# Eight scaled copies of h queued behind the last square of h, at the seam into layer 1's feed-forward

## The chip, the cores and the metric

The kernel runs on one core of a Trainium2 chip. The metric is device time in microseconds, the median of several executions; one further execution was recorded by the hardware profiler and is the source of all times inside the kernel. The engines are named as in the profile: PE (TensorE's matmuls) and PEld (its weight loads), DVE (VectorE), ACT (ScalarE), POOL (GpSimd), SP (SyncE, which issues most DMAs).

## The reference

Two layers over x of 512 rows by 1024 channels. Layer 0 is a convolution module and a feed-forward, layer 1 a windowed attention and a feed-forward; each is added to the running sum h, and a norm ends it. What matters here is the feed-forward of layer 1, with D = 1024 and a hidden width of 2816:

```python
def rmsnorm(x, g):
    xf = x.astype(jnp.float32)
    xf = xf * lax.rsqrt(jnp.mean(xf * xf, axis=-1, keepdims=True) + EPS)
    return (xf * g.astype(jnp.float32)).astype(x.dtype)

def swiglu_ffn(x, w_up, w_down):
    gate, up = jnp.split(x @ w_up, 2, axis=-1)
    return (jax.nn.silu(gate) * up) @ w_down
...
            h = h + attn @ w_o[j]
        h = h + swiglu_ffn(rmsnorm(h, norm_ffn[l]), ffn_w_up[l], ffn_w_down[l])
    return rmsnorm(h, norm_final)
```

## The kernel before

Activations lie transposed: h is eight tiles, h0 to h7, of 128 channels by 512 rows. A product in float32 precision is made of three fast ones (mm3): weights and activations are both split into a rounded high part and a low remainder, and high x high (L356), the weight's high x the activation's low (L357) and the weight's low x the activation's high (L358) are added up in a PSUM bank.

Weights come in chunks of 512 KB in the order of a fixed plan. SP loads a chunk into a raw tile (four of them), ACT casts it to its high part (L273, out whi), DVE subtracts to get the low part (L276, out wlo). A chunk is split up to three uses ahead, into four pairs of tiles, so a cast can wait for PE to be done with an older chunk. Meanwhile sums of weight blocks are made by accumulating DMAs that GpSimd issues (L268).

The norm's factor is applied late: x is h times the norm's gain, and the factor of each row multiplies the result. So the seam from attention to the feed-forward goes like this. The output projection leaves its result in banks and DVE adds it to h (L1410), tile after tile. For each finished tile `Rows.on_h` makes x and adds to the sum of squares: ACT writes the high part of x (L510), DVE the remainder (L511), ACT the square of h (L463), DVE adds it to the squares so far (L467). `Rms.step1` then has PE sum the squares over channels (L477), DVE scale the sum (L479), GpSimd raise it to the power -1/2 (L481) and DVE lay it on a diagonal (L484); `spread` has PE broadcast it (L503).

In layer 1 six of eleven pairs of up-projection tiles are made with seven block products in place of eight. Pair 0 is not: `plain_pair` runs it in four chunks of 24 products, each over half of x's eight tiles. Beside it, `Rows.sums` prepares what the later pairs read: ACT writes eight unrounded scaled copies of h into two tiles f (L726), four to each, and GpSimd makes from them T1 = B11 - B12 (from the first four), T3 = B22 - B12, T2 and T4 (L732). ACT and DVE split each into high and low parts (L518 or L515, and L519 or L516), and the block products read those parts under the name rows.

The order of instructions on each engine is not that of the program text: a planner lays it out when the kernel is built, by a simulated timeline, and each engine then runs its queue strictly in that order. `tc.issue_after(ins)` binds whatever the block under it puts on the engine of `ins` to come after `ins` in that order; it adds no wait on the chip.

The two lines of the seam in which the change lies are `nc.scalar.square(sq, t)` in `Rms.add` and `nc.scalar.mul(f[i // 4][:, i % 4, :], h[i], col(self.gain, i))` in `Rows.sums`.

Of the kernel before, what the change touches and what calls it, by code (L numbers as in the profile page):

```python
# [199 lines left out]
def hybrid_trunk(ctx: ExitStack, tc: tile.TileContext, xT, W, prm_in, wdw_in, sinks, relb, onehot, fin, lead, out):  # L200
    nc = tc.nc
# [10 lines left out]
    def uid(s):  # L212
        ctr[0] += 1
        return f"{s}{ctr[0]}"
# [4 lines left out]
    def quad(dt=F32R):  # L219
        return quads.tile([P, 4, 512], dt, tag="quad", name=uid("quad"))  # L220

    def temp():
        return tmp.tile([P, 512], F32, tag="tmp", name=uid("tmp"))
# [171 lines left out]
    h = [hT[:, i, :] for i in range(KT)]  # L395
# [53 lines left out]
    def col(name, i):  # L449
        c = PARAM_COLS[name] + i  # L450
        return prm[:, c:c + 1]


    class Rms:
# [5 lines left out]

        def add(self, t):
            sq = temp()[:, 0:self.w]
            nc.scalar.square(sq, t)  # L463
            if self.acc is None:
                self.acc = sq
            else:
                self.eng.tensor_add(sq, self.acc, sq)  # L467
                self.acc = sq
# [44 lines left out]
    def split(dst, src, negative=False):  # L513
        if negative:
            nc.scalar.mul(dst[0], src, -1.0)  # L515
            nc.vector.scalar_tensor_tensor(dst[1], src, -1.0, f32(dst[0]), op0=ALU.mult, op1=ALU.subtract)  # L516
            return
        nc.scalar.copy(dst[0], src)  # L518
        nc.vector.tensor_sub(dst[1], src, f32(dst[0]))  # L519
# [190 lines left out]
    class Rows:  # L710
# [12 lines left out]
        def sums(self):  # L723
            f = [quad(F32) for _ in range(2)]
            for i in range(KT):
                nc.scalar.mul(f[i // 4][:, i % 4, :], h[i], col(self.gain, i))  # L726
            b11, b12, b21, b22 = (x[:, :, s] for x in f for s in HALF)
            t1 = self.pool.tile([P, 1024], F32, tag="sum", name=uid("t1"), bufs=1).rearrange("p (k s) -> p k s", k=4)

            for name, t, f, a, b in (("T1", t1, nc.gpsimd.tensor_sub, b11, b12), ("T3", b12, nc.gpsimd.tensor_sub, b22, b12),  # L730
                                     ("T2", b11, nc.gpsimd.tensor_add, b12, b11), ("T4", b21, nc.gpsimd.tensor_sub, b11, b21)):
                f(t, a, b)  # L732
                yield
                both = quads.tile([P, 2, 4, 256], F32R, tag="quad", name=uid("rows"))
                self.block[name] = [both[:, a] for a in range(2)]
                split(self.block[name], t, name == "T2")
# [483 lines left out]
    if True:  # L1220
# [162 lines left out]
        for part in range(2):  # L1383
            for g in range(2):
# [23 lines left out]
                for m in range(4):  # L1408
                    i = g * 4 + m
# [98 lines left out]
```

## Time and profile before

| | us |
|---|---|
| median of 3 executions | 1071.57 |
| lowest and highest | 1064.79, 1073.39 |
| the profiled execution | 1072.48 |
| its span | 1070.1 |
| PE, busy | 1054.9 |
| DVE, busy | 748.5 |
| ACT, busy | 554.1 |
| POOL, busy | 432.8 |

The span runs from the first to the last instruction of the profile; the rest of the execution's time lies around it. Times in rows count from the span's start. A row of the timeline gives start, duration, engine, source line, operation, what is written and read with shapes, a count, and in brackets the engine's idle time before it with what ended it. A row of the waits gives who waited for whom, total time, number of waits, longest one. A row of a line's own view gives a count, shortest, median and longest duration in ns, and the first and last start.

### The profile page before, as it was taken

How to read it: one execution, taken by the hardware profiler on the slowest of the kernel's cores; microseconds unless marked ns; L12 is line 12 of the kernel's file. 1: busy time of each engine (PE TensorE's matmuls, PEld its weight loads, DVE VectorE, ACT ScalarE, POOL GpSimd, SP SyncE). 2: the span in 40 equal slices, each digit the busy share in tenths (PEclk: the TensorE clock that was granted, in tenths of full speed). 3: DMA queues.
4: the chain of work that ended last, by engine and by line, in shares of the span. 5: the costliest groups of instructions: out<-in, count | busy, mean ns of one | idle time of the engine just before them, and what ended most of it. 6: DMA issues, size and time to landing. Idle time of an engine off the chain costs nothing.

```text
span 1070.1 us, 16002 instructions
## 1 busy us (share of the span) xinstructions
PE 1054.9 (99%) x5878; PEld 917.0 (86%) x5878; DVE 748.5 (70%) x1159; ACT 554.1 (52%) x968; POOL 432.8 (40%) x523
## 2 busy tenths in 40 slices
PE   9999999999999999999999999998999999999996
PEld 7888889999988888888888877777989899898985
DVE  3999988977777644444436466487767778768867
ACT  3887888755565333222343565474544355444543
POOL 3999998710321312211212344123532415315401
PEclk9999999999999999999999999998999999999998
DMA  9238046565556777676766444455989655545532
GB/s 356 86 98 98 3 141 214 178 230 184 177 183 191 236 203 211 169 211 190 189 188 188 138 109 137 118 158 158 277 229 332 213 188 179 157 156 177 180 118 79
DMA packets 52059, 187.92 MB, mean 176 GB/s; under 512 B 6188, under 2 KB 12493, under 8 KB 51277
## 3 DMA queue, kind: packets, MB, share of 16 engines
q1 hardware_dynamic: 44924, 162.74, 46.4%
q0 software_dynamic: 6336, 23.07, 12.6%
q8 instruction: 46, 0.75, 0.3%
q10 hardware_dynamic: 720, 1.10, 0.3%
q14 instruction: 33, 0.26, 0.1%
HBM read 181.64 MB, written 51.38 MB: 218 GB/s over the span
## 4 chain that ended last, share of the span: by engine, by line
PE 96%; DVE 2%; ACT 1%; issue 1%; DMA 1%; POOL 0%; SPq 0%
PE bank L356 19%; PE bank L357 19%; PE bank L358 19%; PE bank L906 10%; PE bank L848 9%; PE bank L388 5%; PE bank L354 4%; PE bank L389 3%; PE bank L1304 1%; PE bank L1346 1%; PE bank L1333 1%; PE bank L1004 1%; DMA both<-in_lead_dram 1%; PE bank L894 1%; PE bank L1461 0%
## 5 line engine op out<-in xcount | busy, mean ns | idle before, releaser
L276 DVE TENSOR_TENSOR wlo<-raw,whi 128x1024 fp32r<-128x1024 f32 x219 | 299.7, 1371 | 175.2 <-ACT whi L273 174.1
L273 ACT CAST whi<-raw 128x1024 fp32r<-128x1024 f32 x219 | 229.6, 1049 | 311.7 <-PE bank L357 199.7
L357 PE MATMUL bank<-quad,whi 128*128 128x512 f32 (+1 forms) x1008 | 349.8, 347 | 3.9 <-DVE quad L511 3.9
L356 PE MATMUL bank<-quad,whi 128*128 128x512 f32 (+1 forms) x1008 | 350.1, 348 | 0.0
L358 PE MATMUL bank<-quad,wlo 128*128 128x512 f32 (+1 forms) x1008 | 349.4, 347 | 0.0
L357 PEld LDWEIGHTS bank<-quad,whi 128*128 128x128 f32 x1008 | 191.5, 190 | 27.5 <-DVE quad L511 4.3
L356 PEld LDWEIGHTS bank<-quad,whi 128*128 128x128 f32 x1008 | 191.6, 190 | 24.8 <-issue 1.6
L358 PEld LDWEIGHTS bank<-quad,wlo 128*128 128x128 f32 x1008 | 191.5, 190 | 23.9 <-issue 0.6
L948 POOL TENSOR_TENSOR pr<-pr,pr 128x256 f32<-128x256 f32 x208 | 156.9, 812 | 6.6 <-ACT pr L947 6.6
L955 DVE SCALAR_TENSOR_TENSOR bank<-apad,wdw,bank 128x256 f32<-128x256 f32 x248 | 112.4, 484 | 3.4
L947 ACT ACTIVATE pr<-apad,wdw 128x256 f32<-128x256 f32 x208 | 98.2, 501 | 14.8 <-POOL pr L948 13.0
L906 PE MATMUL bank<-quad,w 128*128 128x256 f32 x448 | 98.7, 380 | 0.0
L906 PEld LDWEIGHTS bank<-quad,w 128*128 128x128 f32 x448 | 84.9, 190 | 11.8 <-DVE bank L955 0.2
L388 PE MATMUL bank<-quad,whi 128*128 128x512 f32 x212 | 75.9, 398 | 0.0
L268 POOL DMA_DIRECT2D sum<-in_W_dram x22 | 18.3, 833 | 123.0 <-DMA sum<-in_W_dram 122.8
L822 POOL TENSOR_TENSOR up<-up 128x256 f32<-128x256 f32 x40 | 44.2, 1114 | 43.0 <-DVE up L768 41.4
L268 POOL DMA_DIRECT2D sum<-sum x22 | 18.0, 818 | 105.8 <-DMA sum<-in_W_dram 104.3
L389 PE MATMUL bank<-quad,wlo 128*128 128x256 f32 x212 | 59.3, 280 | 0.0
L467 POOL TENSOR_TENSOR tmp<-tmp,tmp 128x256 f32<-128x256 f32 (+1 forms) x28 | 27.0, 963 | 79.1 <-ACT tmp L463 62.8
L848 PE MATMUL bank<-wlo,fhi 128*128 128x512 f32 x140 | 55.1, 393 | 0.0
L356 PE MATMUL bank<-rows,whi 128*128 128x256 f32 x192 | 54.6, 285 | 0.0
L358 PE MATMUL bank<-rows,wlo 128*128 128x256 f32 x192 | 54.3, 283 | 0.0
(220 smaller groups left out, 1603.3 us busy)
## 6 DMA issues: line engine op xcount, KB each, us to landing
raw<-in_W_dram SPq DMA_DIRECT2D x187, 512.0 KB, 3.8
sum<-in_W_dram SPq DMA_DIRECT2D x44, 512.0 KB, 5.4
raw<-sum SPq DMA_DIRECT2D x44, 512.0 KB, 3.9
sum<-in_W_dram POOLq DMA_DIRECT2D x22, 512.0 KB, 6.6
sum<-sum POOLq DMA_DIRECT2D x22, 512.0 KB, 6.4
w<-in_W_dram SPq DMA_DIRECT2D x14, 512.0 KB, 9.0
fd<-fs SPq DMA_DIRECT2D x1, 3072.0 KB, 34.1
h<-in_xT_dram SPq DMA_DIRECT2D x8, 256.0 KB, 8.4
```

The lines of the kernel that those rows point to most:

```text
L273: on_act = nc.scalar.copy(hi, src).ins
L276: latest[:] = [on_act, lo_engine[0].tensor_sub(lo, src, f32(hi)).ins]
L356: nc.tensor.matmul(out, w[0], x[0], start=start, stop=False)
L357: nc.tensor.matmul(out, w[0], x[1], start=False, stop=False)
L358: nc.tensor.matmul(out, w[1], x[0], start=False, stop=stop)
L388: nc.tensor.matmul(first[2], first[0], first[1], start=start, stop=False)
L389: nc.tensor.matmul(second[2], second[0], second[1], start=False, stop=stop)
L848: nc.tensor.matmul(out, x, w[:, ws], start=first and e == 0 and i == 0, stop=e == 1 and i == 2, skip_group_check=True)
L906: mm = nc.tensor.matmul(self.pb[:, w * W2:(w + 1) * W2], w1_of(ct, w, k), x[k] if x else xg[k][:, tok], start=k == 0, stop=k == KT - 1)
L947: on_act = nc.scalar.mul(pr, a[:, j:j + W2], tap(j))
L948: on_pool = nc.gpsimd.tensor_add(pr, acc, pr)
L955: on_dve = nc.vector.scalar_tensor_tensor(yt if i == nd - 1 else c, src, tap(i), c if i else self.shift, op0=ALU.mult, op1=ALU.add)
```

## The change

`Rms.add` keeps the square that it has just issued, so that after all eight tiles `squared` is the square of h7. `Rows.sums` issues its eight copies with that square as their predecessor on ACT. The operations and their operands are the same.

```diff
         def add(self, t):
             sq = temp()[:, 0:self.w]
-            nc.scalar.square(sq, t)
+            self.squared = nc.scalar.square(sq, t).ins
...
         def sums(self):
             f = [quad(F32) for _ in range(2)]
             for i in range(KT):
-                nc.scalar.mul(f[i // 4][:, i % 4, :], h[i], col(self.gain, i))
+                with tc.issue_after(self.rms.squared):
+                    nc.scalar.mul(f[i // 4][:, i % 4, :], h[i], col(self.gain, i))
```

## The prediction

> **What bounds the kernel now.** I read the page first, then the list of waits, the windows around the one long wait, and then the timelines of the engines there. From the page, the span and instructions, TensorE's share, and the chain that ended last:
>
> ```profile
> span 1070.1 us, 16002 instructions
> PE 1054.9 (99%) x5878; PEld 917.0 (86%) x5878; DVE 748.5 (70%) x1159; ACT 554.1 (52%) x968; POOL 432.8 (40%) x523
> PE 96%; DVE 2%; ACT 1%; issue 1%; DMA 1%; POOL 0%; SPq 0%
> ```
>
> PE is the bound: an edit on ACT can pay only where PE waits for something ACT holds up. The list of waits of PE has three lines, and one lies at this seam:
>
> ```profile
> PE bank L357 <- DVE quad L511: 3.9, 1, 3.9
> PE bank L894 <- DVE quad L868: 1.2, 1, 1.2
> PE bank L441 <- POOL ones_m L438: 1.1, 1, 1.1
> ```
>
> A product with a low part of x (L357) waited once, 3.9 us, for DVE's remainder (L511). The windows around it; the columns are stretch, length, busy time of PE, PEld, DVE, ACT and POOL, granted clock, DMA share, GB/s:
>
> ```profile
> 721.20:725.08 3.88, 0.00 (x1) 0.00 (x1) 3.88 (x3) 0.00 (x0) 3.20 (x2) 1.00 0.09 38
> 725.08:727.80 2.72, 2.72 (x12) 2.48 (x13) 2.72 (x3) 1.66 (x2) 0.00 (x0) 0.66 0.00 0
> 727.80:732.70 4.90, 4.90 (x13) 3.84 (x14) 4.80 (x5) 1.29 (x2) 4.42 (x2) 0.50 0.71 247
> 732.70:741.10 8.40, 8.40 (x38) 6.95 (x37) 4.09 (x5) 2.01 (x2) 0.89 (x1) 1.00 0.85 213
> ```
>
> PE stands for 3.88 us and then runs at a granted clock of 0.66 and 0.50 before it is back at 1.00. The slow stretches did 2.72 x 0.66 + 4.90 x 0.50 = 4.25 us of full-speed work in 7.62 us: 3.37 us lost. The seam costs 3.88 + 3.37 = **7.25 us**.
>
> Why the remainder is late: ACT's queue, in order.
>
> ```profile
> 709.73 0.71 ACT L510 ACTIVATE quad<-h,prm 128x512 fp32r<-128x512 f32 x1
> 710.34 0.62 ACT L463 ACTIVATE tmp<-h 128x512 f32<-128x512 f32 x1
> 710.87 3.78 ACT L726 ACTIVATE quad<-h,prm 128x512 f32<-128x512 f32 x6
> 714.55 1.03 ACT L273 CAST whi<-raw 128x1024 fp32r<-128x1024 f32 x1
> 715.49 0.72 ACT L510 ACTIVATE quad<-h,prm 128x512 fp32r<-128x512 f32 x1
> 716.12 0.62 ACT L463 ACTIVATE tmp<-h 128x512 f32<-128x512 f32 x1
> 717.25 0.71 ACT L510 ACTIVATE quad<-h,prm 128x512 fp32r<-128x512 f32 x1
> 717.87 0.62 ACT L463 ACTIVATE tmp<-h 128x512 f32<-128x512 f32 x1
> 718.39 0.71 ACT L726 ACTIVATE quad<-h,prm 128x512 f32<-128x512 f32 x1
> 719.94 1.05 ACT L273 CAST whi<-raw 128x1024 fp32r<-128x1024 f32 x1
> ```
>
> Six copies (L726) stand ahead of the high parts (L510) of the last two rows of tiles, h6 and h7. DVE's queue, then GpSimd's:
>
> ```profile
> 710.01 0.68 DVE L1410 TENSOR_TENSOR h<-bank,h 128x512 f32<-128x512 f32 x1
> 711.87 0.68 DVE L1410 TENSOR_TENSOR h<-bank,h 128x512 f32<-128x512 f32 x1
> 712.47 0.68 DVE L467 TENSOR_TENSOR tmp<-tmp,tmp 128x512 f32<-128x512 f32 x1
> 715.62 3.19 DVE L276 TENSOR_TENSOR wlo<-raw,whi 128x1024 fp32r<-128x1024 f32 x1 [2.47 <-ACT whi L273]
> 718.74 0.74 DVE L511 SCALAR_TENSOR_TENSOR quad<-h,prm,quad 128x512 fp32r<-128x512 f32 x1
> 719.40 2.88 DVE L467 TENSOR_TENSOR tmp<-tmp,tmp 128x512 f32<-128x512 f32 x1
> 722.21 2.82 DVE L511 SCALAR_TENSOR_TENSOR quad<-h,prm,quad 128x512 fp32r<-128x512 f32 x1
> 726.69 1.21 DVE L276 TENSOR_TENSOR wlo<-raw,whi 128x1024 fp32r<-128x1024 f32 x1
> 728.00 0.16 DVE L479 TENSOR_SCALAR ms<-bank 128x4 f32<-128x4 f32 x1
> 730.36 2.86 DVE L484 TENSOR_TENSOR tmp<-ident,rs 128x512 f32<-128x512 f32 x1
> ```
>
> ```profile
> 714.49 0.80 POOL L268 DMA_DIRECT2D sum<-sum  x1 [11.19 <-DMA sum<-in_W_dram]
> 715.04 2.68 POOL L732 TENSOR_TENSOR t<-quad 128x1024 f32<-128x1024 f32 x1
> 719.24 2.49 POOL L732 TENSOR_TENSOR quad<-quad,quad 128x1024 f32<-128x1024 f32 x1 [1.52 <-ACT quad L726]
> 721.81 2.67 POOL L732 TENSOR_TENSOR quad<-quad 128x1024 f32<-128x1024 f32 x1
> 728.24 1.97 POOL L481 TENSOR_TENSOR rs<-ms,mhalf 128x4 f32<-128x4 f32 x1 [3.76 <-DVE ms L479]
> 730.19 2.47 POOL L732 TENSOR_TENSOR quad<-quad,quad 128x1024 f32<-128x1024 f32 x1
> ```
>
> h6 and h7 were complete at 710.69 and 712.55 (L1410), yet L510 took them at 715.49 and 717.25. Worse, what DVE then did beside GpSimd's sums (L732) was slow: L276 3.19 us against 1.21, L467 2.88 against 0.68, L511 2.82 against 0.74. The excess is 1.98 + 2.20 + 2.08 = 6.26 us, and the last remainder ended at 725.03. So the early copies hurt twice: they hold ACT, and they let GpSimd's sums start while DVE still prepares x.
>
> **The change part by part.** No instruction is added or removed; eight copies move behind the last square (L463 at 717.87) on ACT's queue.
>
> *ACT.* Without copies ahead, ACT is free at 710.96. L510 and L463 follow one another by 0.61 to 0.63 us. The place of the weight cast L273 isn't fixed by the edit. Were it ahead of h6: cast 710.96 to 712.0, h6's two steps to 713.2, h7's to 714.4 (h7 has been there since 712.55). Were it behind, they end about 0.6 us sooner, held by h7. I take the later. Then the eight copies at 3.78 / 6 = 0.63 us: 714.4 to 719.4, the fourth at 716.9. The last copy ended at 719.10 before, so ACT's later work (L518, L273 at 719.94) moves by some 0.3 us.
>
> *DVE.* After L467 at 712.47 come L276 (1.21, to 714.3), then L511 and L467 twice, at a pitch of about 0.66: remainder of h6 at 715.0, of **h7 at 716.3**, the last sum of squares at 716.9.
>
> *GpSimd.* Its first sum needs four copies, so it starts at 716.9 in place of 715.04, and the second waits for all eight, 719.4. No sum then runs beside the preparation of x. Were two of the five DVE steps caught all the same, at 2.2 us each, h7's remainder would come at 720.7. On GpSimd's queue the DMA issue (L268) stays ahead of the sums, as in the trace; SP's loads are not moved, and the one that waits for the raw tile of L276 can go some 4.5 us sooner (714.3 for 718.81).
>
> *PE.* It reaches the stalled product at 721.20: 4.9 us after 716.3, and still 0.5 us after the caught case. The wait goes, and with it the reason for the slow clock. The Trainium skill, page TensorE: Matmul & The Clock Gate, Part 1, says that the clock falls to half after about one idle window of 3.4 us, free-running. The trace agrees in kind, 3.88 us and then 0.50. By that rule a remaining wait of, say, 2 us would cost just itself.
>
> *What is late next.* Two things behind it, each read against PE 7.25 us earlier:
>
> ```profile
> 726.26 1.70 PE L477 MATMUL bank<-ones_c,tmp 128*128 128x1 f32 x8
> 741.16 1.02 PE L503 MATMUL bank<-tmp,ones_m 128*128 128x512 f32 x2
> L356 PE MATMUL bank<-rows,whi x32: 277/283/368, 745.2 to 764.4; 128*128 128x256 f32 x32
> ```
>
> L477 follows the stalled products by 1.18 us, so about 722.4, and its input is there at 716.9. It ends near 723.3; then DVE's L479, GpSimd's power L481, DVE's L484 and PE's L503, which would fall at 733.9. With the four sums back to back from 716.9 (2.68; 719.6 to 722.1; to 724.8) and L481 behind the third: 726.8, L484 at 2.86: 729.7, 4.2 us to spare. With the fourth sum ahead of L481: 732.2, 1.7 us to spare. The sums' own products (L356 from rows) move from 745.2 to 738.0; the first sum ends near 719.6 and its split needs two operations, so a dozen us are left. Cost: nothing in both, covered by PE's products up to 733.9; if that cover were gone, PE would wait for what the chain overran.
>
> **Sum.** The profiled execution took 1072.48 us, 2.38 above its span. 1072.48 - 7.25 = 1065.2. It lies 0.9 above the median of the runs shown (1071.57), from which the same difference leads to 1064.3. I predict **1065**. The bounds of the gain by rows: 7.25 from above, as PE's other two waits aren't touched; from below zero, where another wait takes its place. I take the upper end since each margin found (4.9, 5.5 and 1.7 to 4.2 us) is positive. The lowest of the three runs shown, 1064.79, is 7.7 below the profiled one; that some executions lack the wait is possible, but no trace shows it.
>
> **Rivals.**
>
> *The wait comes back a little further on.* The order on each engine is laid out by a planner at build time, and the copies' new place can shift L477 or the split of a weight. If PE waits 2 to 4 us at another place, with or without a slow stretch, the time is 1067 to 1073. For it: DVE was busy in 11.40 of the 11.50 us from 721.20 to 732.70 (the windows). Against it: every margin above.
>
> *Slower: the sums pushed onto the scale.* The place is L503. GpSimd's four sums (10.3 us) now fill 716.9 to 729 or so, just when L479, L481 and L484 are due, and DVE has two L276 and two splits of sums there. If these stand ahead and are stretched to 3.19, L479 comes at about 726 in place of 723.3, L481 behind the fourth sum at 729.3, and L484 behind another two at 1.21 ends at 734.6; that alone is a wait of 0.7 us. It decides from 3.9 us on, when L484 ends past 737.8: then the slow stretch comes too, and 5 us of wait make 5 + 3.4 - 7.25 = 1.1 us more, 1073.6; 10 us make 1078.6. The Trainium skill, GPSIMD Engine Reference, Key points, names the contention of GpSimd with DVE's instructions that read two inputs from SBUF, so the collision moves rather than goes; the 3.19, 2.88 and 2.82 above agree. Against it: nothing of PE hangs on DVE's other work there for 10 us.
>
> *The change doesn't bind.* If the remainder of h7 is late through DVE alone, the wait stays: 1071 to 1073. Against it: L276 waited 2.47 us for ACT (its row), and L510 took h7 4.7 us late.
>
> *More than the seam.* The planner may lay out all that follows a little better; PE's 15.2 us outside its busy time less 3.9 bound it. Below 1061 would need several us more.
>
> **How the numbers follow.** Forecast, 1062 to 1068: 0.64. The wait comes back, or the change doesn't bind, 1067 to 1074: 0.18. Slower by the scale, or by another order of the rest: 0.10, half of it beyond 1%. Below 1062: 0.08, of which 0.05 beyond 1%. The range takes the forecast, most of the second case and a spread of executions like that of the runs before: 1061 to 1073. About 1% is what a measurement of this kernel tells from no change; it is 10.7 us, more than the seam holds. So faster by over 1%: 0.05; within 1%: 0.90; slower by over 1%: 0.05.
>
> **What would show it.** Right: the list of PE's waits has no line L357 <- L511, the granted clock stays at 1.00 between 715 and 742, the eight copies stand together behind the last L463, the L511 of h7 takes some 0.74 us and ends before the first L732 starts, and L503 comes some 7 us sooner. Wrong: a new wait of PE at L477 or L503; L732 beside L511 still; a slow stretch elsewhere in layer 1; or a loss on PE that no wait at this seam explains, which would mean that the planner's new order, not the copies, set the time.

## The result, and the profile after

The changed kernel took 1065.12 us (median of 16, 1064.26 to 1066.74) against 1070.94 for the kernel before in the same rounds (16, 1064.79 to 1073.39): a ratio of 0.9953, 95% interval 0.9940 to 0.9967. Predicted were 1065 and "within 1%". The profiled execution took 1065.14 us, 7.34 less than the one before; the medians lie 5.8 apart, because most executions of the kernel before were faster than its profiled one (1072.48), two of the sixteen near 1065. Of all executions in this study one, of a later kernel with copies moved and sums held, took 1772.83 us at a mean granted clock of 0.556, and the ratios leave it out.

The page of the changed kernel, its span and each engine's busy time; under them all of PE's waits longer than a tenth of a microsecond, from the list of waits:

```profile
span 1062.6 us, 16003 instructions
PE 1051.8 (99%) x5878; PEld 914.9 (86%) x5878; DVE 748.1 (70%) x1159; ACT 554.1 (52%) x968; POOL 433.0 (41%) x523
```

```profile
PE bank L441 <- POOL ones_m L438: 1.1, 1, 1.1
PE bank L895 <- DVE quad L869: 0.7, 2, 0.5
```

The wait of L357 for L511 is gone; what is left lies in the first 10 us of the kernel. The windows at the seam (columns as in the prediction) show PE busy throughout at a granted clock of 1.00:

```profile
715.00:721.10 6.10, 6.10 (x29) 5.05 (x28) 2.67 (x4) 6.01 (x9) 4.22 (x2) 1.00 0.70 173
721.10:726.00 4.90, 4.90 (x27) 4.18 (x26) 4.90 (x2) 2.94 (x3) 3.84 (x2) 1.00 0.56 214
726.00:733.60 7.60, 7.60 (x35) 6.28 (x34) 6.66 (x8) 2.24 (x4) 5.17 (x3) 1.00 0.20 22
```

ACT's timeline: the weight cast went ahead of h6, both last rows of x follow at once, and the eight copies (L726 before, L727 now) stand in one block behind the last square.

```profile
710.87 1.05 ACT L273 CAST whi<-raw 128x1024 fp32r<-128x1024 f32 x1
711.83 0.72 ACT L510 ACTIVATE quad<-h,prm 128x512 fp32r<-128x512 f32 x1
712.45 0.62 ACT L463 ACTIVATE tmp<-h 128x512 f32<-128x512 f32 x1
712.97 0.71 ACT L510 ACTIVATE quad<-h,prm 128x512 fp32r<-128x512 f32 x1
713.59 0.62 ACT L463 ACTIVATE tmp<-h 128x512 f32<-128x512 f32 x1
714.11 5.01 ACT L727 ACTIVATE quad<-h,prm 128x512 f32<-128x512 f32 x8
```

From DVE's and GpSimd's timelines (the sums, L732 before, are L733):

```profile
712.91 1.21 DVE L276 TENSOR_TENSOR wlo<-raw,whi 128x1024 fp32r<-128x1024 f32 x1
714.05 0.74 DVE L511 SCALAR_TENSOR_TENSOR quad<-h,prm,quad 128x512 fp32r<-128x512 f32 x1
714.71 0.68 DVE L467 TENSOR_TENSOR tmp<-tmp,tmp 128x512 f32<-128x512 f32 x1
715.31 0.74 DVE L511 SCALAR_TENSOR_TENSOR quad<-h,prm,quad 128x512 fp32r<-128x512 f32 x1
715.97 0.68 DVE L467 TENSOR_TENSOR tmp<-tmp,tmp 128x512 f32<-128x512 f32 x1
720.09 2.68 DVE L276 TENSOR_TENSOR wlo<-raw,whi 128x1024 fp32r<-128x1024 f32 x1 [3.44 <-ACT whi L273]
722.69 3.42 DVE L519 TENSOR_TENSOR rows<-t,rows 128x1024 fp32r<-128x1024 f32 x1
726.03 0.15 DVE L479 TENSOR_SCALAR ms<-bank 128x4 f32<-128x4 f32 x1
728.25 2.90 DVE L484 TENSOR_TENSOR tmp<-ident,rs 128x512 f32<-128x512 f32 x1 [0.94 <-POOL rs L481]
```

```profile
716.80 2.40 POOL L733 TENSOR_TENSOR t<-quad 128x1024 f32<-128x1024 f32 x1 [2.16 <-ACT quad L727]
719.28 2.40 POOL L733 TENSOR_TENSOR quad<-quad,quad 128x1024 f32<-128x1024 f32 x1
721.76 3.26 POOL L733 TENSOR_TENSOR quad<-quad 128x1024 f32<-128x1024 f32 x1
726.26 1.96 POOL L481 TENSOR_TENSOR rs<-ms,mhalf 128x4 f32<-128x4 f32 x1 [1.24 <-DVE ms L479]
```

The five DVE steps in question, one weight remainder (L276) and two steps each for h6 and h7, took 0.68 to 1.21 us and ended at 716.65, before the first sum began at 716.80. The slow DVE steps did not vanish: they are now L276, L519 and L484, with 2.68, 3.42 and 2.90 us. Two later steps of PE, of which the first reads the sum of squares and the second the diagonal that L484 writes:

```profile
721.55 0.95 PE L477 MATMUL bank<-ones_c,tmp 128*128 128x1 f32 x8
733.61 1.02 PE L503 MATMUL bank<-tmp,ones_m 128*128 128x512 f32 x2
```

L503 comes at 733.61 in place of 741.16, 7.55 us sooner. The two traces were 0.17 us apart already before the seam (ACT's cast L273 at 694.71 and 694.54), so the seam gave 7.4 us, and nothing was given back behind it: the spans differ by 7.5.

### The profile page after: what moved, and what is told of

It reads as the page before. It is cut to its first block, busy times and chain, and to the rows that moved or that the text cites. A ratio compares the mean times of both kernels' runs of the same rounds, so it can differ in the third digit from the quotient of the medians.

```text
span 1062.6 us, 16003 instructions
## 1 busy us (share of the span) xinstructions
PE 1051.8 (99%) x5878; PEld 914.9 (86%) x5878; DVE 748.1 (70%) x1159; ACT 554.1 (52%) x968; POOL 433.0 (41%) x523
## 4 chain that ended last, share of the span: by engine, by line
PE 98%; DVE 1%; DMA 1%; ACT 0%; issue 0%; POOL 0%; SPq 0%
PE bank L356 20%; PE bank L358 20%; PE bank L357 20%; PE bank L907 10%; PE bank L849 9%; PE bank L388 5%; PE bank L354 4%; PE bank L389 3%; PE bank L1305 1%; PE bank L1347 1%; PE bank L1334 1%; PE bank L1005 1%; DMA both<-in_lead_dram 1%; PE bank L895 1%; PE bank L1462 0%; PE bank L1426 0%
## 5 line engine op out<-in xcount | busy, mean ns | idle before, releaser
L276 DVE TENSOR_TENSOR wlo<-raw,whi 128x1024 fp32r<-128x1024 f32 x219 | 303.1, 1386 | 169.1 <-ACT whi L273 168.1
L273 ACT CAST whi<-raw 128x1024 fp32r<-128x1024 f32 x219 | 229.7, 1050 | 297.8 <-PE bank L357 189.8
L357 PE MATMUL bank<-quad,whi 128*128 128x512 f32 (+1 forms) x1008 | 348.7, 346 | 0.0
L357 PEld LDWEIGHTS bank<-quad,whi 128*128 128x128 f32 x1008 | 191.0, 189 | 23.2 <-issue 0.2
L467 POOL TENSOR_TENSOR tmp<-tmp,tmp 128x256 f32<-128x256 f32 (+1 forms) x28 | 27.0, 963 | 78.6 <-ACT tmp L463 62.4
```

The lines of the kernel that those rows point to most:

```text
L273: on_act = nc.scalar.copy(hi, src).ins
L276: latest[:] = [on_act, lo_engine[0].tensor_sub(lo, src, f32(hi)).ins]
L357: nc.tensor.matmul(out, w[0], x[1], start=False, stop=False)
```

## The experiments

The theory to be tested has two halves: the early copies keep ACT from h6 and h7, and they let GpSimd's sums start while DVE prepares x. The experiments separate them, then dose the wait itself.

**Only the sums held.** The kernel before, with GpSimd's sums behind a small operation that waits for the last sum of squares; ACT keeps its early copies.

```diff
+            gate = small.tile([P, 4], F32, tag="gate", name=uid("gate"))
+            gated = nc.gpsimd.tensor_add(gate, self.rms.acc[:, 0:4], mhalf).ins
...
-                f(t, a, b)
+                with tc.issue_after(gated):
+                    f(t, a, b)
```

> The kernel before, with GpSimd's four sums held until the last sum of squares is there; ACT's copies stay early. Theory 'collision': the copies ahead of h6 and h7 delay ACT by up to 4.7 us, but that alone fits into PE's cover; the remainder of h7 ends near 718.8 (cast 714.6, L276 to 716.8, then steps of 0.66 us), 2.4 us before PE needs it at 721.2; no wait of PE at L357, no slow clock, 1065 (1064 to 1067). Rival 'ACT's queue': the early copies are enough to make PE wait; the wait of about 3.9 us and the slow clock stay, 1071.

Measured: 1063.80 us, ratio 0.9943 (0.9923 to 0.9962). ACT, DVE and GpSimd at the seam:

```profile
710.25 3.79 ACT L726 ACTIVATE quad<-h,prm 128x512 f32<-128x512 f32 x6
```

```profile
715.01 1.23 DVE L276 TENSOR_TENSOR wlo<-raw,whi 128x1024 fp32r<-128x1024 f32 x1 [2.48 <-ACT whi L273]
717.41 0.75 DVE L511 SCALAR_TENSOR_TENSOR quad<-h,prm,quad 128x512 fp32r<-128x512 f32 x1
719.46 3.02 DVE L276 TENSOR_TENSOR wlo<-raw,whi 128x1024 fp32r<-128x1024 f32 x1 [0.70 <-ACT whi L273]
```

```profile
719.00 2.40 POOL L735 TENSOR_TENSOR t<-quad 128x1024 f32<-128x1024 f32 x1
```

Six copies still stand ahead of h6 on ACT, DVE still waits 2.48 us for the cast, and PE doesn't wait at the seam at all. ACT's delay alone cost PE nothing here. The last two fences show what a collision is: L276 began at 719.46, inside a GpSimd sum that ended at 721.40, and ended at 722.48, 1.08 us after it, a little under the 1.23 that it takes alone. Before, too, L467 and L511 ended 0.55 us after the sums beside them (722.28 and 721.73; 725.03 and 724.48), against 0.68 and 0.74 alone. So the rows read best as a wait: DVE's step does its work once GpSimd's instruction is over, and isn't slowed all along. The Trainium skill, page SBUF — State Buffer, section SBUF: two separate sides, says that the pair of SBUF ports that DVE and GpSimd share is an exclusive lock held for the whole instruction, for DVE operations with two inputs from SBUF against a GpSimd operation that reads SBUF; these rows agree.

**Only the collision.** The changed kernel with three further subtractions on GpSimd, from h7's completion on; they write a tile that is overwritten.

```diff
+            if i == KT - 1:
+                junk = self.pool.tile([P, 1024], F32, tag="sum", name=uid("junk"), bufs=1).rearrange("p (k s) -> p k s", k=4)
+                for _ in range(3):
+                    nc.gpsimd.tensor_sub(junk, hT[:, 4:8, 0:256], hT[:, 4:8, 256:512])
```

> The changed kernel, with three more subtractions of 128x1024 on GpSimd (their result is overwritten and used by nothing) from the moment h7 is complete, 712.4, so that GpSimd is busy for some 7.5 us while DVE prepares x of h6 and h7; the copies stay late. Theory 'collision needs ACT's delay too': DVE runs at about a third of its speed to 720, h7's remainder ends at 720 to 721.5, PE waits 0 to 1 us, no slow clock, 1065 to 1067. Rival 'the collision alone': the wait is as before, 3 to 4 us with the slow clock, 1070 to 1073. By both, DVE's steps take 2 to 3 us each.

Measured: 1072.42 us, ratio 1.0015 (0.9999 to 1.0031): the whole gain is gone. PE's waits, DVE, GpSimd, and one window:

```profile
PE bank L477 <- DVE tmp L467: 1.8, 1, 1.8
PE bank L357 <- DVE quad L511: 1.6, 1, 1.6
```

```profile
713.37 2.91 DVE L511 SCALAR_TENSOR_TENSOR quad<-h,prm,quad 128x512 fp32r<-128x512 f32 x1
716.20 2.90 DVE L467 TENSOR_TENSOR tmp<-tmp,tmp 128x512 f32<-128x512 f32 x1
719.02 2.86 DVE L511 SCALAR_TENSOR_TENSOR quad<-h,prm,quad 128x512 fp32r<-128x512 f32 x1
721.80 2.85 DVE L467 TENSOR_TENSOR tmp<-tmp,tmp 128x512 f32<-128x512 f32 x1
```

```profile
712.75 8.58 POOL L725 TENSOR_TENSOR junk<-h 128x1024 f32<-128x1024 f32 x3
721.41 2.70 POOL L737 TENSOR_TENSOR t<-quad 128x1024 f32<-128x1024 f32 x1
```

```profile
723.28:730.11 6.83, 5.40 (x17) 4.63 (x18) 4.85 (x4) 1.79 (x2) 4.08 (x3) 0.50 0.46 154
```

Here ACT was early and the collision alone made PE wait, 1.6 and 1.8 us; the granted clock fell to 0.50 at 723.28, inside the second wait. The rival held: 3.4 us of wait in two pieces, the slow clock, and a time within its 1070 to 1073. What was expected as "a third of its speed" was strict alternation: one DVE step, one GpSimd instruction, four times over (the fourth with the first real sum), about 2.8 us for each pair.

**How many turns fit.** A turn is one DVE step held up by one GpSimd instruction. Two kernels: in the first, only the last four copies are bound; in the second, the kernel before holds all sums but the first.

```diff
-                with tc.issue_after(self.rms.squared):
+                with tc.issue_after(self.rms.squared) if i >= 4 else nullcontext():
```

> The changed kernel with only the last four copies bound behind the last square; the first four, and so GpSimd's first sum, may go early. Theory 'turns' (a DVE step that meets a GpSimd sum waits for its end and then runs at its own speed, one sum for each step caught): one sum is early, one step is caught, 2.1 us; h7's remainder ends at 719 to 720, PE needs it near 721; no wait, clock 1.00, 1065 (1064 to 1066). Rival 'any early copy costs': a wait of PE of 1 us or more, and 1068 to 1072.

```diff
-                with tc.issue_after(gated):
+                with tc.issue_after(gated) if name != "T1" else nullcontext():
```

> The kernel before, ACT's copies early, GpSimd's first sum free and the other three held until the last sum of squares. Theory 'turns': the first sum catches L276, which ends near 718.8 as before; then L511, L467, L511 run at 0.66 us each and h7's remainder ends near 720.8, 0.4 us before PE needs it: no wait or under 0.5 us, 1064 to 1067. Rival 'the first sum is what matters': the wait stays above 2 us, 1069 to 1072.

Measured: 1065.72 us, ratio 0.9958 (0.9939 to 0.9976), and 1064.64 us, 0.9942 (0.9925 to 0.9959). DVE and GpSimd in the first, then in the second:

```profile
715.31 2.90 DVE L511 SCALAR_TENSOR_TENSOR quad<-h,prm,quad 128x512 fp32r<-128x512 f32 x1
719.39 2.89 DVE L467 TENSOR_TENSOR tmp<-tmp,tmp 128x512 f32<-128x512 f32 x1
714.64 3.02 POOL L733 TENSOR_TENSOR t<-quad 128x1024 f32<-128x1024 f32 x1
```

```profile
716.17 2.77 DVE L276 TENSOR_TENSOR wlo<-raw,whi 128x1024 fp32r<-128x1024 f32 x1 [2.47 <-ACT whi L273]
720.12 0.74 DVE L511 SCALAR_TENSOR_TENSOR quad<-h,prm,quad 128x512 fp32r<-128x512 f32 x1
715.16 2.68 POOL L735 TENSOR_TENSOR t<-quad 128x1024 f32<-128x1024 f32 x1
```

With one turn lost ahead of it, h7's remainder came in time in both (719.47 and 720.86), although in the second ACT's six copies stood in front again. In the first, where one caught step was expected, the second sum caught the last sum of squares (L467) too, and PE waited 0.5 us at L477; its times are uneven, two of ten near 1070. One turn fits into PE's cover; the kernel before lost three.

**The wait by itself.** The changed kernel with further copies on ACT, used by nothing, between the square of h6 and the high part of h7: seven, then eleven, then six.

```diff
+            hold = nullcontext()
+            if i == KT - 1:
+                junk = self.pool.tile([P, 1024], F32, tag="sum", name=uid("junk"), bufs=1)
+                with tc.issue_after(self.rms.squared):
+                    for _ in range(7):
+                        held = nc.scalar.mul(junk, hT[:, 0:2, :].rearrange("p k s -> p (k s)"), col(self.gain, 0)).ins
+                hold = tc.issue_after(held)
+            with hold:
+                split_scaled(self.x[i], h[i], col(self.gain, i))
+                self.rms.add(h[i])
```

> The changed kernel, with seven further copies of 128x1024 on ACT (used by nothing) between the square of h6 and the high part of h7, about 0.95 us each; nothing runs on GpSimd at that time. h7's remainder ends at about 722.1, PE waits about 1.1 us (0.5 to 2). Theory 'a short wait keeps the clock': the granted clock stays at 1.00 and the time is 1066 to 1067.5. Rival 'each wait is paid twice': the slow stretch follows a short wait too, 3.4 us on top, 1069 to 1071.

> As the one with seven copies on ACT, with eleven: PE waits about 4.9 us (4 to 6). Theory 'a long wait is paid twice': a stretch of granted clock 0.50 follows, of 6.8 us as before, 3.4 us lost, 1072 to 1075. Rival 'the slow clock came of the collision, not of the wait': 4.9 us alone, 1069 to 1071, clock at 1.00.

> As the one with seven further copies on ACT, with six: PE's wait falls by one copy, 1.17 us, from 2.1 to about 0.9 us. Theory 'every wait of PE here brings the slow clock': granted clock 0.50 for 6.8 us, 3.4 us lost, 1068 to 1070. Rival 'it takes more than a microsecond': clock 1.00, 1065.5 to 1067.

Measured: 1069.83 us, ratio 1.0007 (0.9990 to 1.0024), with seven; 1075.80, 1.0050 (1.0035 to 1.0065), with eleven; 1069.64, 0.9984 (0.9967 to 1.0001), with six. PE's waits and, under them, the windows behind them, first with seven, then eleven, then six:

```profile
PE bank L356 <- ACT quad L510: 2.1, 1, 2.1
```

```profile
723.80:730.70 6.90, 6.90 (x21) 5.74 (x22) 1.80 (x3) 6.30 (x10) 5.53 (x4) 0.51 0.50 77
```

```profile
PE bank L356 <- ACT quad L510: 6.8, 1, 6.8
```

```profile
727.40:736.60 9.20, 9.17 (x26) 7.45 (x27) 4.23 (x4) 7.64 (x12) 6.04 (x4) 0.50 0.24 47
```

```profile
PE bank L356 <- DVE tmp L775: 2.3, 1, 2.3
...
PE bank L356 <- ACT quad L510: 0.9, 1, 0.9
```

```profile
721.00:728.00 7.00, 6.95 (x34) 5.53 (x35) 3.11 (x4) 6.20 (x10) 3.69 (x3) 1.00 0.51 116
745.00:748.40 3.40, 3.40 (x18) 3.40 (x17) 3.40 (x4) 3.40 (x7) 2.48 (x3) 0.50 0.68 128
```

The waits were longer than expected (2.1 and 6.8 us for 1.1 and 4.9), for the most part because a copy took 1.17 us, not 0.95. A wait of 2.1 us was followed by 6.9 us at half the clock: "a short wait keeps the clock" fell. With eleven, too, the slow clock came with the wait although no step of DVE had met a GpSimd sum up to there: so the wait brings it, not the collision. With six, 0.9 us of wait left the clock at 1.00, as the rival had it; yet the time is no better, for PE waited another 2.3 us, up to 744.44, for the first pair's banks, which DVE had still to read (L775), with 3.4 us of half clock behind that. The time fell into the range of the theory that the clock refutes, by this other wait, which neither had foreseen. So very late copies can make PE wait at a second place; the changed kernel stays clear of it.

**Held sums against moved copies.** The first experiment came out 1.3 us under the change, in other rounds and with overlapping intervals. Three kernels in shared rounds: it, the change, and both edits together; then the change with a small tile that nothing reads.

> The kernel before with GpSimd's four sums held, a second time, to set it beside the changed kernel in shared rounds. If holding the sums is better than moving the copies: 1063.8, 1.3 us under the changed kernel, as in its first run. If that was a matter of executions: 1065, within 0.5 us of the changed kernel.

> The changed kernel as it is, beside the other two of these rounds, for comparison: 1065.1, as in its first runs.

> The changed kernel with GpSimd's sums held besides. No step of DVE is caught before h7's remainder in either, so by the collision alone it equals the changed kernel: 1065, no wait of PE at the seam. If the held sums help in themselves: 1063.8, as the kernel before with held sums.

```diff
             self.rms = Rms(new_bc(), ALL, nc.vector)
+            nc.gpsimd.memset(small.tile([P, 4], F32, tag="pad", name=uid("pad")), 0.0)
```

> The changed kernel with one more small tile (128 x 4, four buffers, 128 bytes in each partition) that nothing reads; GpSimd's sums are not held. The three kernels with held sums have such a tile too, and in them the remainder tile of the odd down-projection pairs lies 128 bytes further and the matmuls of that stage go 0.227 us apart where the changed kernel has 0.226 to 0.236. Theory 'placement': 1063.8, with 0.227 between those matmuls, 1 to 1.6 us under the changed kernel. Rival 'the held sums': 1065.1 to 1065.4, as the changed kernel.

Measured in shared rounds: 1064.43 us with the sums held, ratio 0.9954 (0.9938 to 0.9970); 1065.41 for the change, 0.9971 (0.9954 to 0.9988); 1063.76 with both, 0.9951 (0.9933 to 0.9969). The change with the unread tile, in other rounds: 1064.39 (six runs), 0.9947 (0.9932 to 0.9962), span 1060.8. The times alone can't separate these, as the intervals overlap; the traces can. The first and the last kind of the down-projection's matmuls, first in the changed kernel, then with the unread tile:

```profile
L849 PE MATMUL bank<-whi,fhi x140: 389/389/397, 779.9 to 1047.0; 128*128 128x512 f32 x140
L849 PE MATMUL bank<-whi,flo x140: 387/393/404, 780.3 to 1047.5; 128*128 128x512 f32 x140
```

```profile
L850 PE MATMUL bank<-whi,fhi x140: 389/389/396, 779.3 to 1045.2; 128*128 128x512 f32 x140
L850 PE MATMUL bank<-whi,flo x140: 389/389/389, 779.7 to 1045.7; 128*128 128x512 f32 x140
```

The sums are not held there, and the stage from the first to the last of these starts is 1.2 us shorter all the same: 266.4 us for 267.6. It takes 266.4 us in each of the five traces with an added small tile, whatever the seam does, and 267.6 or 267.7 in each of the eight without, the kernel before among them. So the last microsecond isn't the seam's: it goes with the added tile. That the remainder tile of the odd pairs thereby lies 128 bytes further, and that this is the cause, no trace shows; that part is argued. The kernel with the lowest median in the shared rounds holds the change, the held sums and the added tile together; it lies 1.65 us under the change alone there, and beside the unread tile alone it can't be told apart.

## Why the prediction was right, point by point

*The bound and the price of the seam.* Right. 7.25 us were read out of the trace (3.88 of wait, 3.37 of slow clock); the seam gave 7.4, and the profiled execution came to 1065.14 where the sum said 1065.2. That the median (1065.12) met the 1065 so closely is in part luck: the same sum from the median shown led to 1064.3, and the medians differ by 5.8, not 7.25. And "about 1%" as what a measurement of this kernel tells from no change was too coarse: with an interval of 0.9940 to 0.9967 a change of half a percent is told from none.

*ACT.* Right, with the later of the two places for the cast: the copies ran from 714.11 to 719.12, predicted 714.4 to 719.4.

*DVE and GpSimd.* Right for the change: h7's remainder at 716.05 (predicted 716.3), the last sum of squares at 716.65 (716.9), the first GpSimd sum at 716.80 (716.9).

*"So the early copies hurt twice."* Half wrong. ACT's delay cost nothing alone (held sums: no wait at L357 with the copies still early), and one collision fits as well. The collisions, three of them, are what made PE wait, and they can do so without ACT's delay (the load on GpSimd).

*"Were two of the five DVE steps caught all the same ..."* The size was wrong as a bound: it added 2.2 us twice and found 0.5 us to spare. The load on GpSimd caught four steps, since each step that meets a running GpSimd instruction loses the rest of it, and the two alternate as long as both have work.

*The clock.* The row was read rightly, the use of the rule wasn't. The prediction inferred from the Trainium skill's page TensorE: Matmul & The Clock Gate, Part 1, that "a remaining wait of, say, 2 us would cost just itself"; 2.1 us were followed by 6.9 us at 0.51, and 1.6 us, with 1.8 to follow, by 6.83 at 0.50. Only the waits of 0.5 and 0.9 us were not followed by it. The measurement decides; the forecast did not rest on it, but the rival's price did ("It decides from 3.9 us on"), and was too low between 2 and 3.9 us.

*What is late next.* Right in size, not by its path. L484 ended at 731.15, within the predicted 729.7 to 732.2, and L503 at 733.61 (733.9) had 2.5 us to spare. But L479 came at 726.03, not at about 723.3: L519 stood ahead of it and waited for GpSimd's third sum, and GpSimd was idle for 1.24 us until L479 let L481 go. That step, with its time ("about 726"), is the rival's, "the sums pushed onto the scale"; the collisions moved to L276, L519 and L484 as it said. It stopped short of PE because L481 was not pushed behind the fourth sum as well (726.26, the fourth began at 728.20). With six more copies on ACT the same stage did make PE wait, 2.3 us, one step further on.

*The distance between medians.* The prediction left open whether some executions of the kernel before lack the wait. Some took 1064.8 to 1066.4 us in every set of rounds but the last (2 of 16, 3 of 24, 1 of 25, 8 of 29, 0 of 11). For the last four sets each execution's mean granted clock is on record: these twelve had 0.997 or 0.998, as the changed kernel has in its sixteen, while 68 of the other 77 had 0.992 to 0.996 and the profiled one 0.994. A stretch of 6.83 us at half clock lowers the mean by 0.003. So these twelve by all appearance ran without the slow stretch, and some executions of the kernel before escape what the change removes. Why, no trace shows, as none was taken of such an execution; the turns may have fallen otherwise, for in the profiled one GpSimd's second sum began at 719.24, only 0.16 us ahead of DVE's L467.

## What to carry to other kernels

When a producer step that should take 0.7 us takes 2.9, look at GpSimd's timeline beside it before blaming the queue that feeds it: if the step always ends the same time after a GpSimd instruction, as here 0.55 or 1.08 us, the two take turns, and the cure is to keep GpSimd's optional work out of that stretch, on whichever engine this is easiest to order. Price a wait of PE with the slow clock that follows, from the granted clock in the windows: here it nearly doubled the loss. And before crediting a last microsecond to an edit, compare the stages that the edit should not touch: here a stage of 267 us changed by 1.2.

## What was not expected of the hardware

A wait of PE of 2.1 us was enough for some 6.8 us at half the clock, and so were 1.6 us and, 1.0 us of work later, the start of a second wait; 0.9 us alone was not. A DVE operation of 128x4 with a single tensor input was held as well: with the sums held, the one that negates the scale took 2.83 us beside a GpSimd sum, 0.16 in the changed kernel. And one small tile that nothing reads went with 4 ns on the median of one kind of matmul, 393 to 389, and 1.2 us on a stage of 420 matmuls.
